# Conditioning tiles in buffers of their own, loaded two ahead and dealt out twice per block, in a two-layer encoder kernel; the first transfers in one queue; x times rstd formed once

## The chip, the core and the metric

The kernel runs on one core of a Trainium2 chip. The core has five engines with instruction streams of their own: TensorE (PE, matmul into the PSUM memory), VectorE (DVE), ScalarE (ACT), GpSimd (POOL) and SyncE (SP, which here only issues DMA transfers). Each works through its own list in order and waits for the others by semaphores. The metric is the time on the device of one execution, in microseconds (us). The kernel before took 959.88 us in the median of three runs (955.91 to 963.48).

## What is computed

A trunk of two layers over 256 tokens of width 1024. Each layer is half a gated feed-forward, a token mixer, and another half feed-forward; shift, scale and gate of each of the three norms come from one condition vector `c` by a matrix `mod_w` of 1024 x 9216 per layer:

```python
c_act = jax.nn.silu(c)
for i in range(DEPTH):                     # 2
    mod = (c_act @ mod_w[i] + mod_b[i])[:, None, :]
    sh0, sc0, g0, sh1, sc1, g1, sh2, sc2, g2 = jnp.split(mod, N_MOD, axis=-1)
    h = modulate(rms_norm(x, norm_g[i, 0]), sh0, sc0)      # h * (1 + scale) + shift
    x = x + 0.5 * g0 * swiglu(h, ffn_w_gu[i, 0], ffn_w_down[i, 0])
    h = modulate(rms_norm(x, norm_g[i, 1]), sh1, sc1)
    ...                                    # layer 0: pooling mixer, layer 1: differential attention
    x = x + g1 * y
    h = modulate(rms_norm(x, norm_g[i, 2]), sh2, sc2)
    x = x + 0.5 * g2 * swiglu(h, ffn_w_gu[i, 1], ffn_w_down[i, 1])
return rms_norm(x, final_g)
```

`swiglu` multiplies by a 1024 x 5632 matrix, takes `silu(g) * u`, and multiplies by a 2816 x 1024 matrix. All is float32.

## The kernel before

The activations stay on the chip, transposed: `xT` holds x as eight row blocks of 128 channels by 256 tokens. All weights are streamed once, in 312 units of 128 x 1024 (48 of them 128 x 768) in the order of use. A float32 product is made of three fast ones: each unit is split by ACT into a rounded part `hi` (L285) and by DVE into the remainder `lo` (L286), as are the activations (`hh`, `hl`, or `ah`, `al`), and `prod3` (L305 to L307) adds hi x hi, hi x lo and lo x hi in PSUM.

**The order of the work.** `split_unit` issues the load of a unit on SP's queue into the pool `rawp` (six raw buffers) and splits it; `unit` keeps five units ahead of the one in use, and there are seven buffers each for `hi` and `lo`. The instructions are placed on each engine by a scheduler at build time that goes by priority and by when it reckons inputs to be ready; on the chip each engine then follows that order.

**The conditioning.** The product of `c` with `mod_w` is done by DVE, in 144 tiles of 128 rows (`gemv_tile`, L243): a tile is loaded into a raw buffer of the same pool `rawp` (L247), and one instruction multiplies it with `cact` (silu of c in every partition) and sums each row into a column of `mod` (L248), followed by a short read-out of the sum. `mod_done` adds the bias and forms what the norm or the residual needs: `A` (scale with the norm's gain), `sh`, or the gate `G`. Eight tiles make one part of 1024 columns, 18 parts in all. Parts (0, 0) and (0, 1), shift and scale of the first norm, are made in the opening stage, row block by row block. The others are dealt out by `Background`: `tick` is called once per block of the up projection (11 blocks of 256 columns of gate and of up) and once per unit of the down projection, and does as many tiles as are then due.

**The stages.** The opening stage (L781 to L812) forms the first norm and, for each row block k, a tile of scale, a tile of shift, the normalised block, and the products with two units of 128 x 768 for the first three up blocks (`early`). Then come: feed-forward (0, 0) with its remaining eight up blocks and its down projection, the pooling mixer, feed-forwards (0, 1) and (1, 0), attention, feed-forward (1, 1). A down projection runs in four quarters of 256 output columns, six units each; after a quarter, `residual` (L372, then L314 and L315 for the scaled and split x of the next norm) and `squares` (L382, L383) add to x and to the sum of squares `acc`. At the start of a feed-forward or of attention `rstd_rows` sums `acc` over partitions on PE (L353). The first up blocks there do not wait for the norm: they multiply by x times gain, `xh` and `xl` (L408 to L410), and the factor `rstd` comes afterwards.

In this text the boundary after a down projection is where PE goes over to those products; the first of the two that the trace singles out lies between feed-forwards (0, 1) and (1, 0), the second between (1, 0) and attention.

Of the kernel before, what the change touches and what calls it, by code (L numbers as in the profile page):

```python
# [18 lines left out]
P = 128  # L19
# [11 lines left out]
RAW_BUFS = 6  # L31
SPLIT_BUFS = 7
LOOKAHEAD = 5
U_BUFS = 3
EARLY = 3

# [66 lines left out]

VECTORS = [("modb0", 72), ("ng0", 24), ("pscale", 8), ("modb1", 72), ("ng1", 24), ("fg", 8), ("subln", 1)]
# [32 lines left out]
def trunk(ctx: ExitStack, tc: tile.TileContext, x, c, mod_w, small, weights, diff_lambda, k_rope, out):  # L137
# [52 lines left out]
    for _ in range(10):  # L190
        PE.matmul(pt[:, :P], ones, ones, start=True, stop=True)
# [11 lines left out]


    cact = const([P, D], "cact")
# [9 lines left out]
    S.activation(cact, cact, AF.Silu)  # L215
# [5 lines left out]
    def mod_done(i, p, k0=0, k1=KD):  # L221

        n, ks = p // 3, slice(k0, k1)
        cs = slice(p * 8 + k0, p * 8 + k1)
# [6 lines left out]
        if key not in vecs:  # L231
            vecs[key] = const([P, KD], f"{key[0]}{i}{p}")
        v = vecs[key][:, ks]
        if p % 3 == 1:
            V.scalar_tensor_tensor(v, m, 1.0, vec[f"ng{i}"][:, n * 8 + k0:n * 8 + k1], ALU.add, ALU.mult)
        elif n != 1:
            V.tensor_scalar(v, m, 0.5, None, ALU.mult)
        elif i == 0:
            V.tensor_tensor(v, m, vec["pscale"][:, ks], ALU.mult)
        else:  # L240
            V.tensor_copy(v, m)

    def gemv_tile(i, p, k):  # L243

        raw = rawp.tile([P, D], F32, tag="raw", name=nm("raw"))
        r0 = (p * KD + k) * P
        nc.sync.dma_start(raw, mod_w[i, r0:r0 + P, :])  # L247
        V.scalar_tensor_tensor(raw, raw, 1.0, cact, ALU.mult, ALU.mult, accum_out=mod[i][:, p * KD + k:p * KD + k + 1])  # L248

    def gemv_steps(i, p):  # L250
        for k in range(KD):
            gemv_tile(i, p, k)
# [85 lines left out]
    def warm(f, after):  # L338

        S.activation(tiny(1, tag="warm", bufs=1), after, f, scale=0.0, bias=eps1)  # L340

# [48 lines left out]
    def normalise(js, rstd, a, b):  # L390

        with tc.high_priority(offset=100):
            for j in js:
                t = t1k()
                first = V.scalar_tensor_tensor(t, xT[:, j, :], a[:, j:j + 1], rstd, ALU.mult, ALU.mult)
                second = S.activation(hh[:, j, :], t, AF.Identity, bias=b[:, j:j + 1])
                V.scalar_tensor_tensor(hl[:, j, :], t, b[:, j:j + 1], hh[:, j, :].bitcast(F32), ALU.add, ALU.subtract)
        return first.ins, second.ins
# [56 lines left out]
    def ffn(i, s, ndef, nxt, parts_up, parts_down, early=()):  # L455
# [6 lines left out]
        back = Background(parts_up, KF // 2, ndef + len(early) // 2)  # L462
        for j in range(KF // 2):
            if (i, s, j) == (1, 0, 6):
                attention_consts()
            if j >= ndef:
# [37 lines left out]
            normalise(range(j * n, j * n + n), rstd, vecs["A", i, n3], b)  # L504
            back.tick()
# [274 lines left out]

    with tc.high_priority(offset=1000):  # L781
        pt = psmall()
        for half in range(2):
            sq = t1k(1024, "qk", 2)
            S.activation(sq, xT[:, 4 * half:4 * half + 4, :].rearrange(F), AF.Square)
            for k in range(4):
                PE.matmul(pt[:, :T], ones, sq[:, k * T:(k + 1) * T], start=(half + k == 0), stop=(half + k == 4))
        rstd = norm_of(pt, t1k(T, "pk", 1))
# [12 lines left out]
    on_v, on_s = scale_and_shift(0)  # L801
    for k in range(KD):
        with tc.issue_after(on_v), tc.issue_after(on_s):
            prefetch(2)
            if k < KD - 1:
                on_v, on_s = scale_and_shift(k + 1)
# [6 lines left out]
    ffn(0, 0, 0, ("A", 0, 1), [(0, 2), (0, 4), (0, 3), (0, 5)], [(0, 7), (0, 6)], early)  # L813
    pool_mixer(("A", 0, 2))
    ffn(0, 1, 2, ("A", 1, 0), [(0, 8), (1, 1)], [(1, 0), (1, 4)])
# [58 lines left out]
```

## Time and profile before

| what | value |
|---|---|
| median of three runs | 959.88 us (955.91 to 963.48) |
| the profiled execution | 959.34 us, of which 957.5 us are the span from first to last instruction |
| PE busy | 912.9 us, 95% of the span, 7504 matmuls |
| DVE busy | 743.9 us, 78% |
| ACT busy | 492.2 us, 51% |
| mean granted clock of PE | 0.982 |
| read from memory, mean rate | 234.86 MB, 249 GB/s with the writes |

Busy shares are means over stages with different limits; PE's matmuls are pipelined, so that a busy PE shows only that it always had one in flight. The granted clock is given as a share of 2.4 GHz; its two levels here are 1.00 and 0.50 (1.2 GHz). In rows of waits, the part before the arrow waited for the part behind it. In rows in order of time, the bracket gives the idle time ahead of the instruction and what ended it.

### The profile page before, as it was taken

The numbers are of one execution on the slowest core, as the hardware profiler recorded it, in microseconds if no ns is written. First come the engines' busy times: TensorE is split into PE (matmuls) and PEld (weight loads), VectorE is DVE, ScalarE is ACT, GpSimd is POOL, SyncE is SP. The second block draws the span as 40 slices with busy tenths as digits, with TensorE's granted clock in tenths as the row PEclk, the third lists the DMA queues.
The fourth block names the chain that finished last, engine by engine and source line by source line (L and its number), as shares of the span: only waits on it lengthen the run. The fifth ranks groups of instructions, "written<-read, shape, count | busy, mean of one in ns | idle before, by whom it ended". The sixth has DMA issues, their size and how long they took to land.

```text
span 957.5 us, 18703 instructions
## 1 busy us (share of the span) xinstructions
PE 912.9 (95%) x7504; PEld 898.8 (94%) x7504; DVE 743.9 (78%) x1238; ACT 492.2 (51%) x745; POOL 0.7 (0%) x6
## 2 busy tenths in 40 slices
PE   5999999998999999997999999969999999999997
PEld 4889999998999999997999999859999999999996
DVE  4899988898998666787997767688988897665551
ACT  3364444546745444355654434347777674444541
POOL 0000000000000000000000000000000000000000
PEclk7999999999999999998999999979999999999999
DMA  6989998997569878887698887894543448776621
GB/s 253 322 315 359 363 333 308 362 328 261 176 234 365 261 240 266 276 300 237 215 339 300 291 280 249 272 310 147 161 142 121 154 155 286 240 228 199 182 78 45
DMA packets 68583, 238.18 MB, mean 249 GB/s; under 512 B 7952, under 2 KB 9232, under 8 KB 68368
## 3 DMA queue, kind: packets, MB, share of 16 engines
q1 hardware_dynamic: 68208, 235.41, 72.1%
q8 instruction: 59, 0.97, 0.4%
q10 hardware_dynamic: 288, 1.57, 0.4%
q14 instruction: 28, 0.23, 0.1%
HBM read 234.86 MB, written 1.05 MB: 246 GB/s over the span
## 4 chain that ended last, share of the span: by engine, by line
PE 72%; DMA 12%; DVE 10%; issue 5%; ACT 1%; DVEq 0%; ACTq 0%
PE mm L305 17%; PE mm L307 17%; PE mm L306 16%; DMA raw<-in_mod_w_dram 10%; DVE lo L286 4%; PE hd L305 3%; PE hd L307 3%; PE hd L306 3%; PE mm L409 2%; PE mm L410 2%; PE mm L408 2%; DVE raw L248 2%; PE hd L618 1%; DMA raw<-in_weights_dram 1%; DMA xT<-in_x_dram 1%
## 5 line engine op out<-in xcount | busy, mean ns | idle before, releaser
L285 ACT ACTIVATE hi<-raw 128x1024 fp32r<-128x1024 f32 (+1 forms) x312 | 315.7, 1024 | 265.2 <-PE mm L306 108.3
L286 DVE TENSOR_TENSOR lo<-raw,hi 128x1024 fp32r<-128x1024 f32 (+1 forms) x312 | 362.9, 1180 | 69.6 <-ACT hi L285 66.9
L305 PE MATMUL mm<-hh,hi 128*128 128x256 f32 x992 | 277.8, 281 | 0.0
L306 PE MATMUL mm<-hl,hi 128*128 128x256 f32 x992 | 277.6, 281 | 0.0
L307 PE MATMUL mm<-hh,lo 128*128 128x256 f32 x992 | 275.8, 281 | 0.0
L248 DVE SCALAR_TENSOR_TENSOR raw<-raw,cact 128x1024 f32<-128x1024 f32 x144 | 174.3, 1222 | 79.8 <-DMA raw<-in_mod_w_dram 79.5
L307 PE MATMUL mm<-ahl,lo 128*128 128x256 f32 x768 | 216.1, 281 | 5.1 <-DVE lo L286 5.1
L305 PE MATMUL mm<-ahl,hi 128*128 128x256 f32 x768 | 215.6, 281 | 0.0
L306 PE MATMUL mm<-ahl,hi 128*128 128x256 f32 x768 | 215.3, 280 | 0.0
L305 PEld LDWEIGHTS mm<-hh,hi 128*128 128x128 f32 x992 | 186.7, 188 | 0.8
L306 PEld LDWEIGHTS mm<-hl,hi 128*128 128x128 f32 x992 | 186.9, 189 | 0.0
L307 PEld LDWEIGHTS mm<-hh,lo 128*128 128x128 f32 x992 | 185.9, 189 | 0.3
L307 PEld LDWEIGHTS mm<-ahl,lo 128*128 128x128 f32 x768 | 144.6, 188 | 6.6 <-DVE lo L286 6.5
L305 PEld LDWEIGHTS mm<-ahl,hi 128*128 128x128 f32 x768 | 144.6, 188 | 0.3 <-DVE xT L372 0.2
L306 PEld LDWEIGHTS mm<-ahl,hi 128*128 128x128 f32 x768 | 144.7, 188 | 0.0
L305 PE MATMUL hd<-hh,hi 128*128 128x256 f32 x288 | 81.5, 283 | 4.5 <-ACT hi L285 4.3
L307 PE MATMUL hd<-hh,lo 128*128 128x256 f32 x288 | 82.1, 285 | 3.5 <-DVE lo L286 3.2
L306 PE MATMUL hd<-hl,hi 128*128 128x256 f32 x288 | 81.1, 282 | 0.0
L410 PE MATMUL mm<-xh,lo 128*128 128x258 f32 x208 | 60.2, 291 | 1.9 <-DVE lo L286 1.9
L409 PE MATMUL mm<-xl,hi 128*128 128x256 f32 x208 | 61.4, 296 | 0.2 <-DVE xl L315 0.2
L408 PE MATMUL mm<-xh,hi 128*128 128x258 f32 x208 | 59.9, 291 | 0.1
L305 PEld LDWEIGHTS hd<-hh,hi 128*128 128x128 f32 x288 | 54.5, 189 | 5.7 <-ACT hi L285 5.7
(190 smaller groups left out, 1022.2 us busy)
## 6 DMA issues: line engine op xcount, KB each, us to landing
raw<-in_weights_dram SPq DMA_DIRECT2D x264, 512.0 KB, 4.8
raw<-in_mod_w_dram SPq DMA_DIRECT2D x144, 512.0 KB, 5.4
raw<-in_weights_dram SPq DMA_DIRECT2D x48, 384.0 KB, 4.6
xT<-in_x_dram ACTq DMA_DIRECT2D x1, 1024.0 KB, 8.3
out_dram<-u SPq DMA_DIRECT2D x4, 256.0 KB, 2.4
cact<-in_c_dram ACTq DMA_DIRECT2D x1, 512.0 KB, 4.7
pk<-qk SPq DMA_DIRECT2D x16, 32.0 KB, 2.8
qk<-pk SPq DMA_DIRECT2D x16, 32.0 KB, 1.8
```

Of the source, the lines that this page charges most:

```text
L248: V.scalar_tensor_tensor(raw, raw, 1.0, cact, ALU.mult, ALU.mult, accum_out=mod[i][:, p * KD + k:p * KD + k + 1])
L285: S.activation(hi[:, :w], raw[:, :w], AF.Copy)
L286: V.tensor_tensor(lo[:, :w], raw[:, :w], hi[:, :w].bitcast(F32), ALU.subtract)
L305: PE.matmul(o, lh, rh, start=start, stop=False, **kw)
L306: PE.matmul(o, lh, rl, start=False, stop=False, **kw)
L307: PE.matmul(o, ll, rh, start=False, stop=stop, **kw)
L408: PE.matmul(o[:, :T + 2], hi[:, kk, cs], xh[:, k, :], start=(k == 0), stop=False)
L409: PE.matmul(o[:, :T], hi[:, kk, cs], xl[:, k, :], start=False, stop=False)
L410: PE.matmul(o[:, :T + 2], lo[:, kk, cs], xh[:, k, :], start=False, stop=(k == KD - 1))
L618: PE.matmul(sc[c2][:, q * T:(q + 1) * T], l[pr, 0, qs], r[pr, 1, :], start=(n == 0), stop=(n == 2))
```

## The change

- The loads of x (in two halves) and of `c` are issued on SP's queue ahead of all others; the small vectors go to ACT's queue instead. `warm` (an activation of one column, which makes the activation table load early) is called for Silu and for the reciprocal root in the opening.
- The matmuls on ones at the start are 12 instead of 10, and 12 more stand between the sum of squares and the first product.
- In the opening, x times rstd is formed once per block by DVE (`scaled_x`: one block, one, two, then four in one instruction); ACT forms the block's `A` and `sh` columns and twice the normalised block (`h` in full and `hh` rounded), and DVE subtracts. Before, DVE formed `A`, `sh` and `t`, ACT `hh`, and DVE the difference.
- Conditioning tiles have three buffers of their own (tag `cond`). `gemv_load` issues loads from one list of all tiles in the order of use, in the background up to two tiles beyond the one in use; in the opening a tile is loaded just when it is used.
- `Background` has 22 ticks per up projection instead of 11: one behind the gate product and one behind the up product of each block.
- The weights' pools shrink: five raw buffers instead of six, six `hi` and `lo` buffers instead of seven, four units ahead instead of five.

```diff
-RAW_BUFS = 6
-SPLIT_BUFS = 7
-LOOKAHEAD = 5
+RAW_BUFS = 5
+SPLIT_BUFS = 6
+LOOKAHEAD = 4
+COND_BUFS = 3
+WARM = 12
...
     cact = const([P, D], "cact")
-    nc.scalar.dma_start(cact, c.broadcast_to([P, D]))
-    nc.scalar.dma_start(xT, x)
+    for half in range(2):
+        hs = slice(half * KD // 2, (half + 1) * KD // 2)
+        nc.sync.dma_start(xT[:, hs, :], x[:, hs, :])
+    nc.sync.dma_start(cact, c.broadcast_to([P, D]))
...
-    nc.sync.dma_start(vecT, small)
+    nc.scalar.dma_start(vecT, small)
...
+    tiles = iter([(0, p, k) for k in range(KD) for p in (1, 0)] + [(*part, k) for part in PARTS for k in range(KD)])
+    loaded = []
+
+    def gemv_load(n):
+        while len(loaded) < n:
+            nxt = next(tiles, None)
+            if nxt is None:
+                return
+            i, p, k = nxt
+            raw = rawp.tile([P, D], F32, tag="cond", name=nm("cond"), bufs=COND_BUFS)
+            r0 = (p * KD + k) * P
+            nc.sync.dma_start(raw, mod_w[i, r0:r0 + P, :])
+            loaded.append((nxt, raw))
+
+    def gemv_tile(i, p, k, out, ahead_=COND_BUFS):
 
-        raw = rawp.tile([P, D], F32, tag="raw", name=nm("raw"))
-        r0 = (p * KD + k) * P
-        nc.sync.dma_start(raw, mod_w[i, r0:r0 + P, :])
-        V.scalar_tensor_tensor(raw, raw, 1.0, cact, ALU.mult, ALU.mult, accum_out=mod[i][:, p * KD + k:p * KD + k + 1])
+        gemv_load(ahead_)
+        which, raw = loaded.pop(0)
+        assert which == (i, p, k)
+        return V.scalar_tensor_tensor(raw, raw, 1.0, cact, ALU.mult, ALU.mult, accum_out=out)
...
-        back = Background(parts_up, KF // 2, ndef + len(early) // 2)
+        back = Background(parts_up, KF, 2 * ndef + len(early))
...
                     mm_rows(pg, hh, hl)
+                back.tick()
                 S.activation(w[:, :512], pg, AF.Silu)
...
     def scale_and_shift(k):
+        ks = slice(k, k + 1)
         for p in (1, 0):
-            gemv_tile(0, p, k)
-            mod_done(0, p, k, k + 1)
-        return normalise([k], rstd, vecs["A", 0, 0], mod[0][:, 0:8])
+            last = gemv_tile(0, p, k, d[:, p, ks], 1)
+        S.activation(a0[:, ks], d[:, 1, ks], AF.Identity, scale=ng[:, ks], bias=b1[:, ks])
+        S.activation(sh0[:, ks], d[:, 0, ks], AF.Identity, bias=vec["modb0"][:, ks])
+        xk = xr[k // 4][:, k % 4 * T:(k % 4 + 1) * T]
+        h = t1k()
+        with tc.high_priority(offset=100):
+            S.activation(h, xk, AF.Identity, scale=a0[:, ks], bias=sh0[:, ks])
+            second = S.activation(hh[:, k, :], xk, AF.Identity, scale=a0[:, ks], bias=sh0[:, ks])
+            third = V.tensor_tensor(hl[:, k, :], h, hh[:, k, :].bitcast(F32), ALU.subtract)
+        return last.ins, second.ins, third.ins
```

**SP's queue at the start of the program.** Before, it opens with the small vectors and two conditioning tiles (`raw` from `in_mod_w`), then two weight units; x and c are issued by ACT at that time:

```order
L210 DMA vecT<-in_small_dram 128x209
L247 DMA raw_139<-in_mod_w_dram 128x1024
L247 DMA raw_145<-in_mod_w_dram 128x1024
L282 DMA raw_153<-in_weights_dram 128x768
L282 DMA raw_159<-in_weights_dram 128x768
L247 DMA raw_165<-in_mod_w_dram 128x1024
L247 DMA raw_170<-in_mod_w_dram 128x1024
```

In the changed kernel:

```order
L218 DMA xT<-in_x_dram 128x1024 x2
L219 DMA cact<-in_c_dram 128x1024
L268 DMA cond_166<-in_mod_w_dram 128x1024
L268 DMA cond_169<-in_mod_w_dram 128x1024
L310 DMA raw_178<-in_weights_dram 128x768
L310 DMA raw_184<-in_weights_dram 128x768
L268 DMA cond_191<-in_mod_w_dram 128x1024
L268 DMA cond_194<-in_mod_w_dram 128x1024
```

Three transfers have moved to the head of the queue, and one has left it.

**DVE ahead of the last residual of feed-forward (0, 1)**, the first of the two boundaries (`lo` are splits, `xT` is the residual of the last quarter, `raw` or `cond` with `mod` in the row is a conditioning product). Before:

```order
L248 SCALAR_TENSOR_TENSOR raw_5060,mod_106<-raw_5060,cact 128x1024
L248 SCALAR_TENSOR_TENSOR raw_5087,mod_106<-raw_5087,cact 128x1024
L286 TENSOR_TENSOR lo_5002<-raw_5000,hi_5001 128x1024
L226 TENSOR_TENSOR mod_106<-mod_106,vecT 128x8
L286 TENSOR_TENSOR lo_5032<-raw_5030,hi_5031 128x1024
L235 SCALAR_TENSOR_TENSOR A_5091<-mod_106,vecT 128x8
L286 TENSOR_TENSOR lo_5065<-raw_5063,hi_5064 128x1024
L286 TENSOR_TENSOR lo_5095<-raw_5093,hi_5094 128x1024
L286 TENSOR_TENSOR lo_5150<-raw_5148,hi_5149 128x1024
L372 SCALAR_TENSOR_TENSOR xT<-mm_4933,G_3689,xT 128x256 x2
```

In the changed kernel:

```order
L276 SCALAR_TENSOR_TENSOR cond_6115,mod_113<-cond_6115,cact 128x1024
L314 TENSOR_TENSOR lo_5021<-raw_5019,hi_5020 128x1024
L314 TENSOR_TENSOR lo_5051<-raw_5049,hi_5050 128x1024
L276 SCALAR_TENSOR_TENSOR cond_6183,mod_113<-cond_6183,cact 128x1024
L276 SCALAR_TENSOR_TENSOR cond_6186,mod_113<-cond_6186,cact 128x1024
L314 TENSOR_TENSOR lo_5084<-raw_5082,hi_5083 128x1024
L241 TENSOR_TENSOR mod_113<-mod_113,vecT 128x8
L314 TENSOR_TENSOR lo_5114<-raw_5112,hi_5113 128x1024
L276 SCALAR_TENSOR_TENSOR cond_6251,mod_113<-cond_6251,cact 128x1024
L314 TENSOR_TENSOR lo_5169<-raw_5167,hi_5168 128x1024
L396 SCALAR_TENSOR_TENSOR xT<-mm_4952,G_3708,xT 128x256 x2
```

Four products stand in this quarter instead of two, spread among the five splits instead of ahead of them; they belong to feed-forward (1, 0).

**DVE ahead of the last residual of feed-forward (1, 0)**, the second boundary. Before:

```order
L248 SCALAR_TENSOR_TENSOR raw_7421,mod_106<-raw_7421,cact 128x1024
L248 SCALAR_TENSOR_TENSOR raw_7448,mod_106<-raw_7448,cact 128x1024
L286 TENSOR_TENSOR lo_7363<-raw_7361,hi_7362 128x1024
L226 TENSOR_TENSOR mod_106<-mod_106,vecT 128x8
L286 TENSOR_TENSOR lo_7393<-raw_7391,hi_7392 128x1024
L286 TENSOR_TENSOR lo_7426<-raw_7424,hi_7425 128x1024
L286 TENSOR_TENSOR lo_7454<-raw_7452,hi_7453 128x1024
L286 TENSOR_TENSOR lo_7506<-raw_7504,hi_7505 128x1024
L372 SCALAR_TENSOR_TENSOR xT<-mm_7294,G_5884,xT 128x256 x2
```

In the changed kernel:

```order
L314 TENSOR_TENSOR lo_7382<-raw_7380,hi_7381 128x1024
L314 TENSOR_TENSOR lo_7412<-raw_7410,hi_7411 128x1024
L314 TENSOR_TENSOR lo_7445<-raw_7443,hi_7444 128x1024
L314 TENSOR_TENSOR lo_7473<-raw_7471,hi_7472 128x1024
L314 TENSOR_TENSOR lo_7525<-raw_7523,hi_7524 128x1024
L396 SCALAR_TENSOR_TENSOR xT<-mm_7313,G_5903,xT 128x256 x2
```

The two products in front are gone; the five splits and the residual remain in their order.

## Rows read from the trace of the kernel before

**Rows 1.** The span, from the head of the page.

```profile
span 957.5 us, 18703 instructions
```

**Rows 2.** Stretches, PE alone, then all: busy (instructions), PEclk, DMA share, GB/s.

```profile
10.00:16.00 6.00, 5.44 (x16) 0.65 1.03 406
16.00:20.00 4.00, 0.03 (x1) 1.00 0.04 15
...
20.00:62.00 42.00, 37.88 (x274) 34.66 (x275) 38.06 (x79) 16.75 (x25) 0.00 (x0) 0.96 0.90 313
62.00:151.00 89.00, 89.00 (x760) 89.00 (x760) 81.56 (x113) 44.53 (x54) 0.00 (x0) 1.00 0.95 347
```

**Rows 3.** The opening in order of time (start, length, instruction, idle before); x's landing.

```profile
10.56 5.47 PE L787 MATMUL st<-qk,ones 128*128 128x256 f32 x16 [5.67 <-ACT qk L785]
16.07 0.43 DVE L344 TENSOR_SCALAR t<-st 128x256 f32<-128x256 f32 x1 [4.00 <-PE st L787]
20.18 0.39 PE L305 MATMUL hd<-hh,hi 128*128 128x256 f32 x1 [4.14 <-ACT hi L285]
59.31 2.96 DVE L286 TENSOR_TENSOR lo<-raw,hi 128x768 fp32r<-128x768 f32 x3 [0.25 <-ACT hi L285]
...
xT<-in_x_dram ACTq DMA_DIRECT2D x1, 1024.0 KB, 8.3
```

**Rows 4.** The first boundary in order of time, DVE and PE.

```profile
422.26 0.87 DVE L372 SCALAR_TENSOR_TENSOR xT<-mm,G,xT 128x256 f32<-128x256 f32 x2
431.63 3.49 DVE L286 TENSOR_TENSOR lo<-raw,hi 128x1024 fp32r<-128x1024 f32 x3
435.03 0.87 DVE L372 SCALAR_TENSOR_TENSOR xT<-mm,G,xT 128x256 f32<-128x256 f32 x2
...
431.92 0.28 PE L408 MATMUL mm<-xh,hi 128*128 128x258 f32 x1
438.16 1.22 PE L353 MATMUL st<-acc,ones 128*128 128x256 f32 x2 [5.95 <-DVE acc L383]
```

**Rows 5.** DVE's waits for tiles, 376 to 438 us, then whole; a tile's median landing.

```profile
DVE raw L248 <- DMA raw<-in_mod_w_dram: 13.2, 9, 2.8
...
DVE raw L248 <- DMA raw<-in_mod_w_dram: 79.5, 50, 4.2
...
raw<-in_mod_w_dram SPq DMA_DIRECT2D x144, 512.0 KB, 5.4
```

**Rows 6.** PE's waits, 262 to 660, then 62 to 220: total, times, longest.

```profile
PE st L353 <- DVE acc L383: 13.0, 2, 7.1
PE mm L307 <- DVE lo L286: 3.3, 3, 1.3
PE mm L410 <- DVE lo L286: 1.9, 1, 1.9
...
PE mm L307 <- DVE lo L286: 1.8, 3, 1.0
```

**Rows 7.** Stretches behind the boundaries, columns as in the second of rows 2.

```profile
438.20:444.20 6.00, 6.00 (x26) 5.82 (x27) 3.14 (x8) 1.08 (x2) 0.00 (x0) 0.50 0.81 305
446.20:452.20 6.00, 6.00 (x53) 6.00 (x52) 4.01 (x9) 2.99 (x5) 0.00 (x0) 1.00 0.58 178
641.70:645.40 3.70, 3.70 (x15) 3.52 (x16) 2.74 (x7) 0.42 (x1) 0.00 (x0) 0.50 0.87 355
```

**Rows 8.** DVE's groups by shape: busy, mean ns of one; its busy time 445 to 570.

```profile
L286 DVE TENSOR_TENSOR lo<-raw,hi 128x1024 fp32r<-128x1024 f32 x264 | 318.2, 1221 | 58.6 <-ACT hi L285 55.9 <-DMA pk<-qk 1.7
L248 DVE SCALAR_TENSOR_TENSOR raw<-raw,cact 128x1024 f32<-128x1024 f32 x144 | 174.3, 1222 | 79.8 <-DMA raw<-in_mod_w_dram 79.5
L286 DVE TENSOR_TENSOR lo<-raw,hi 128x768 fp32r<-128x768 f32 x48 | 45.1, 954 | 11.1 <-ACT hi L285 11.0
L372 DVE SCALAR_TENSOR_TENSOR xT<-mm,G,xT 128x256 f32<-128x256 f32 x44 | 19.4, 478 | 17.0 <-PE mm L307 17.0
...
445.00:570.00 125.00, 102.13 (x157) 1.00 0.81 274
```

More of the change, by code (lines that the diff above doesn't have):

```diff
@@ L101, in unit_shape @@
     return (ix[-2].stop - ix[-2].start) // P, ix[-1].stop - ix[-1].start
+UP = [[(0, 2), (0, 4), (0, 3), (0, 5)], [(0, 8), (1, 1)], [(1, 2), (1, 3), (1, 5)], [(1, 8)]]
+DOWN = [[(0, 7), (0, 6)], [(1, 0), (1, 4)], [(1, 7), (1, 6)], []]
+PARTS = [part for up, down in zip(UP, DOWN) for part in up + down]
 VECTORS = [("modb0", 72), ("ng0", 24), ("pscale", 8), ("modb1", 72), ("ng1", 24), ("fg", 8), ("subln", 1)]
@@ L189, in trunk @@
     pt = psum()
-    for _ in range(10):
+    for _ in range(WARM):
         PE.matmul(pt[:, :P], ones, ones, start=True, stop=True)
@@ L394, in normalise @@
                 t = t1k()
[L395 to L396 removed]
+                V.scalar_tensor_tensor(t, xT[:, j, :], a[:, j:j + 1], rstd, ALU.mult, ALU.mult)
+                S.activation(hh[:, j, :], t, AF.Identity, bias=b[:, j:j + 1])
                 V.scalar_tensor_tensor(hl[:, j, :], t, b[:, j:j + 1], hh[:, j, :].bitcast(F32), ALU.add, ALU.subtract)
[L398 removed]
     def mm_deferred(os_):
@@ L504, in ffn @@
             normalise(range(j * n, j * n + n), rstd, vecs["A", i, n3], b)
+            back.tick()
             back.tick()
@@ L777, in attention @@
                     normalise((j, j + 1), rstd, vecs["A", 1, 1], b)
+    xr = [t1k(1024, "qk", 2) for _ in range(2)]
     with tc.high_priority(offset=1000):
@@ L787, in trunk, with scaled_x @@
                 PE.matmul(pt[:, :T], ones, sq[:, k * T:(k + 1) * T], start=(half + k == 0), stop=(half + k == 4))
+        idle = psmall()
+        for _ in range(WARM):
+            PE.matmul(idle[:, :P], ones, ones, start=True, stop=True)
         rstd = norm_of(pt, t1k(T, "pk", 1))
-    early = [psum2(), psum2()] + [psum() for _ in range(2 * EARLY - 2)]
+    def scaled_x(k0, k1):
+        n, o = k1 - k0, k0 % 4 * T
+        V.tensor_tensor(xr[k0 // 4][:, o:o + n * T].rearrange("p (k t) -> p k t", k=n), xT[:, k0:k1, :],
+                        rstd.rearrange("p (o t) -> p o t", o=1).broadcast_to([P, n, T]), ALU.mult)
+    with tc.high_priority(offset=1000):
+        scaled_x(0, 1)
+    early = [psum2(), psum2()] + [psum() for _ in range(2 * EARLY - 2)]
+    b1, d = const([P, KD], "b1"), const([P, 2, KD], "d")
+    a0 = vecs["A", 0, 0] = const([P, KD], "A00")
+    sh0 = vecs["sh", 0, 0] = mod[0][:, 0:KD]
+    ng = vec["ng0"][:, 0:KD]
+    V.scalar_tensor_tensor(b1, vec["modb0"][:, KD:2 * KD], 1.0, ng, ALU.add, ALU.mult)
     def scale_and_shift(k):
+        ks = slice(k, k + 1)
         for p in (1, 0):
-            gemv_tile(0, p, k)
-            mod_done(0, p, k, k + 1)
-        return normalise([k], rstd, vecs["A", 0, 0], mod[0][:, 0:8])
-    on_v, on_s = scale_and_shift(0)
+            last = gemv_tile(0, p, k, d[:, p, ks], 1)
[8 more added lines that the diff above has]
+        return last.ins, second.ins, third.ins
+    on_v, on_s, after = scale_and_shift(0)
     for k in range(KD):
```

41 lines of the change are left out of this document (22 added, 19 removed).

## The prediction

> **What bounds the kernel now.** I read the span first [rows 1], then TensorE's (PE's) waits, because everything in the program ends up feeding it. PE is the bound almost everywhere: from 62 to 151 us it is busy in all of the 89 us and issues 760 matmuls, one per 0.117 us, at full clock [rows 2]. What can be won lies where PE stands still or runs at its lower clock level, and that is in few places.
>
> The first is the start. PE does its first useful product at 20.18 us, and the last weights of the opening stage are split only at about 61 us (the stretch at 59.31 us holds three splits of 0.96 us, of which two belong to that stage) [rows 3]. DMA, the loads of that stage, runs at 406 GB/s from 10 to 16 us, then almost stops (15 GB/s) until 20 us, and afterwards moves 313 GB/s [rows 2]: the six raw buffers are full and nothing frees them until the norm is there. The norm is late because x is: its transfer takes 8.3 us to land, and VectorE (DVE) then waits 4.00 us for PE's sum of squares until 16.07 us [rows 3].
>
> The others are the two boundaries at which a down projection ends, and the down projections before them. At the first, PE stops at 432.2 and waits 5.95 us for the sum of squares; the chain of DVE shows why: the residual of the previous quarter ran at 422.26 us, then came two conditioning products (which wait for their DMA), and five splits, so that the last residual began at 435.03 us, although PE had its input ready before 432 us [rows 4]. The time DVE lost there is the waiting for conditioning tiles: 13.2 us in 9 waits from 376 to 438 us [rows 5]. A tile of `mod_w` takes a raw buffer of the weights' pool and is used by DVE right behind its load in program order, so DVE stands for most of the 5.4 us of its landing [rows 5]. At the second boundary PE waits 1.9 and 7.1 us, and three times before it, 3.3 us together [rows 6]. After each boundary PE's granted clock is 0.50, its level of 1.2 GHz: 26 matmuls in 6.0 us instead of 53 is a loss of 6.0 x 27/53 = 3.0 us; at the second, 15 in 3.7 us instead of 33, 2.0 us [rows 7]. So 5.95 + 3.0 = 9.0 us hang on the first boundary, 1.9 + 7.1 + 2.0 = 11.0 us on the second, 3.3 us on the waits between, and 1.8 us on three short waits in the first down projection [rows 6].
>
> **The start, part by part.** Moving x and c ahead of all else in SP's queue puts 1.57 MB first; the small vectors move to ScalarE's (ACT's) queue, where their only early reader (one 128x8 operation of DVE) stands ahead of a product that cannot begin before about 8 us anyway. A 512 KB tile takes 5.4 us to land [rows 5], so I put the second half of x at 6 us instead of 9.4. ACT squares, PE adds (5.5 us, at the half clock [rows 2, 3]) and the ACT table of the reciprocal root is now loaded before it is asked for. The norm chain and the first product come 3.5 to 5 us earlier. Then DVE's work per row block shrinks: `t` (0.48 us, like the other 256-wide products) and three tiny operations go eight times; four multiplies of x by rstd come, 0.48 us for a 256-wide one, at most 1.22 us for the widest, 2.6 us in all [rows 8]. Counting starts and not ends, since neighbours overlap by some 0.07 us, that is 8 x 0.6 - 2.6 = 2.2 us less. ACT gets three small operations per block, but is busy in 16.75 of 42 us there [rows 2]. Together 5.7 to 7.2 us. The loads allow it: 16.4 MB are needed by the end of the stage, which at 347 GB/s [rows 2] takes 47 us, ending near 50 and not 58. I take **-6.5**, between -2 (if the loads go on at the rate of now and only the standstill shrinks) and -10 (the whole standstill and all of DVE's saving).
>
> The twelve extra matmuls on ones between the squares and the first product, and the two of the start-up, stand where PE is idle now (16 to 20 us, 0.03 us busy [rows 2]): nothing.
>
> A rule of the Trainium skill speaks against the queue part: the page "DMA: Bandwidth & Descriptors", section "Issuing engines are not separate DMA queues", says that transfers of all issuing engines run on the same 16 DMA engines and interleave, so the choice of queue only moves issue time. By that alone x would land where it does now, the start would give some 3 us, and the whole would come to 937 us. No run here shows it; I hold to the order of issue, because x now shares those engines with six loads that SP issues beside it.
>
> **The conditioning tiles.** They get three buffers of their own and are loaded up to two ahead, dealt out per half block. The number of products stays 144 and the bytes stay. The order shows that they run ahead: behind the opening's 16, the numbers that DVE does with the weights of up and down of the four feed-forwards were 24, 20 | 15, 15 | 24, 16 | 8, 0 and become 28, 19 | 24, 19 | 30, 5 | 0, 0 (the rest in the mixers). The last quarter of the third down projection has none any more, so the second boundary and the three waits before it lose their cause: **-10** of 11.0 (bounds -5, if five splits in front of the residual are late for other reasons, and -11) and **-3** of 3.3 (bounds 0 and -3.3).
>
> The first boundary is less sure, as four products now stand in its last quarter instead of two. A quarter of DVE's work: four 1024-wide splits, two 768-wide, and six 256-wide operations, 4 x 1.22 + 2 x 0.95 + 6 x 0.48 = 9.7 us, and 1.3 us per product with its read-out (1.22 and a little) [rows 8]: 14.9 us with four, 16.2 with five, less 1.2 us of overlap. PE needs 132 x 0.117 = 15.4 us. So DVE fits, with 0.4 to 1.7 us to spare, if its waits of 13.2 us in four quarters [rows 5] go; loaded two ahead, a tile has two products' distance (some 6.5 us) against 5.4 us of landing. I take **-7.5** of 9.0 (bounds 0 and -9.0). The short waits of the first down projection: **-1** (0 to -1.8).
>
> **What is given back.** One raw and one split buffer less means weights only four units ahead instead of five, some 11 us of PE work, still twice the landing. In the first up projection the loads are near their limit: eight half-megabyte loads (4.2 MB) in a block of 96 x 0.117 = 11.2 us are 374 GB/s, against 347 GB/s measured there at a DMA share of 0.95 and 406 GB/s at the best [rows 2]. Starting it earlier leaves less in hand. I allow **+2** (0 to 8).
>
> Sum: -6.5 - 1 - 7.5 - 3 - 10 + 2 = -26 on the span of 957.5 us: 931.5, and 1.84 us lie outside the span in that run (959.34, by 0.5 us below the median 959.88): 933.3, given as **933.5 us**.
>
> **Rivals.** *x lands no earlier.* If transfers issued later overtake the two halves of x as those beside it do now, the norm stays at 18 us and the start gives DVE's 2.2 us and some 0.8 from the extra buffers: 937. For it: 8.3 us for 1 MB now; against it: the later ones are now issued behind it. *The loads set the opening.* If 347 GB/s is what DMA gives, the 28 products and 32 units of the first up projection, 60 x 0.524 = 31.5 MB, take 90.7 us where 56 took 84.6, and 6 of the 6.5 us go back: 939. For it: share 0.95; against it: 406 GB/s before. *The first boundary stays.* Nineteen products in that down projection instead of 15 keep DVE late: 933.5 + 7.5 = 941; with waits of 2 us a quarter it would come so. *The waits move along.* The change doesn't do what it says: SP issues in order, a load of weights that waits for one of five raw buffers holds the tile's load behind it, and DVE waits as now, only elsewhere; with the start alone, 953. Against it: the tiles no longer need a raw buffer. *Slower*: the products drawn ahead into the second feed-forward (24 + 19 where 30 were) wait there for DMA by 1.5 us each. At the mean wait of now, 13.2/9 = 1.5 us [rows 5], a quarter of its down projection costs DVE 13.6 + 4.75 x 1.5 = 20.7 against PE's 15.4 us; four quarters lose 21 us where 9.0 were lost, and the third up projection with 30 products another 30 x 1.5 less its slack of 23 us (DVE is busy in 102 of 125 us there [rows 8]), 22 us more: 959 less the 21 of the other terms, plus 12 and 22, is 972. It turns slower at about 1.25 us a product (16 - 9 + 14.5 = 21.5); it needs loads two ahead to gain nothing, which the 5.4 us of landing speak against.
>
> **Chances.** The forecast 0.56 (its own range 922 to 941), x no earlier 0.06, the loads 0.12, the boundary 0.13, moved along 0.07, slower 0.06. Low end: every term at its far bound without the give-back is -10 - 1.8 - 9 - 3.3 - 11 = -35, 924, and 922 with a margin for the pool mixer; high end 948, the two middle rivals together. A change of 1% is about what a measurement of this kernel can tell: faster 0.85, same 0.09, slower 0.06.
>
> **What would show it.** First useful product near 15 to 16 us and no standstill of DMA at 16 to 20; block 3 starting some 6 us sooner; DVE's waits for `mod_w` well under half of 79.5 us [rows 5]; no wait of PE at the second boundary, at most 2 us at the first; clock 1.00 behind both. I am wrong if the waits of PE on splits appear in the second or third feed-forward, if DVE's waits for tiles stay, or if the opening ends where it did.

## The result, and the profile after

The changed kernel takes 951.06 us in the median of 20 runs (947.03 to 958.03), the kernel before 959.77 (952.87 to 963.48); the ratio is 0.992, with a 95% interval of 0.990 to 0.994. The change gains 8.7 us, where 26 were forecast, and lies above the forecast range. The profiled execution took 958.03 us, the longest of them; a second profile of the same kernel (e11, below) took 950.73 us and shows the same waits, so both are used.

The stretches of [rows 2], in the changed kernel (PE, PEld, DVE, ACT, POOL busy with their instructions, PEclk, DMA share, GB/s):

```profile
10.00:16.00 6.00, 2.72 (x25) 2.52 (x23) 4.33 (x9) 3.53 (x8) 0.00 (x0) 0.90 0.98 353
16.00:20.00 4.00, 2.93 (x12) 2.64 (x12) 3.90 (x8) 2.70 (x6) 0.00 (x0) 0.50 0.86 280
20.00:62.00 42.00, 37.62 (x289) 36.77 (x290) 35.08 (x53) 26.73 (x47) 0.00 (x0) 0.94 0.90 311
62.00:151.00 89.00, 86.82 (x725) 85.40 (x724) 79.28 (x111) 40.74 (x48) 0.00 (x0) 1.00 0.93 341
```

The standstill of DMA from 16 to 20 us is gone (280 GB/s instead of 15). But in the first up projection, where PE had been busy without a break, it now does 725 matmuls instead of 760. The opening in order of time, then x's landing among the DMA issues (KB each, median us), answer to [rows 3]:

```profile
6.32 3.72 PE L813 MATMUL st<-u,ones 128*128 128x256 f32 x16 [0.65 <-ACT u L811]
16.86 0.58 PE L333 MATMUL hd<-hh,hi 128*128 128x256 f32 x1 [4.14 <-ACT hi L313]
54.75 0.58 ACT L846 ACTIVATE hh<-qk,mod,A 128x256 fp32r<-128x256 f32 x1
...
10.46 1.23 DVE L276 SCALAR_TENSOR_TENSOR cond<-cond,cact 128x1024 f32<-128x1024 f32 x1 [4.84 <-DMA cond<-in_mod_w_dram]
11.61 0.42 DVE L368 TENSOR_SCALAR t<-st 128x256 f32<-128x256 f32 x1
```

```profile
xT<-in_x_dram SPq DMA_DIRECT2D x2, 512.0 KB, 5.0
```

The sum of squares begins at 6.32 instead of 10.56 us and ends at 10.04 instead of 16.03; the first product comes at 16.86 instead of 20.18. The sum is 6.0 us earlier, the product only 3.3: DVE was in a conditioning product when the sum was ready and took it up at 11.61 us, and a second product (11.94 to 13.16 us) stands ahead of the rest of the norm. The first boundary, DVE and PE in order of time, then the stretch behind it, answer to [rows 4, 7]:

```profile
441.68 1.23 DVE L276 SCALAR_TENSOR_TENSOR cond<-cond,cact 128x1024 f32<-128x1024 f32 x1 [2.31 <-DMA cond<-in_mod_w_dram]
...
449.25 0.87 DVE L396 SCALAR_TENSOR_TENSOR xT<-mm,G,xT 128x256 f32<-128x256 f32 x2
...
452.37 1.22 PE L377 MATMUL st<-acc,ones 128*128 128x256 f32 x2 [10.02 <-DVE acc L407]
```

```profile
452.40:458.40 6.00, 6.00 (x26) 5.82 (x27) 3.91 (x10) 1.06 (x2) 0.00 (x0) 0.50 0.89 302
```

PE waits 10.02 us there, not 5.95 (7.87 in the second profile), again for DVE's last residual, and loses as much clock behind it. What DVE waits for, from 376 to 452 us and then whole, answers to [rows 5] (total, times, longest):

```profile
DVE cond L276 <- DMA cond<-in_mod_w_dram: 12.5, 11, 2.3
...
DVE cond L276 <- DMA cond<-in_mod_w_dram: 47.8, 41, 4.8
```

PE's waits from 440 to 700 us, to be set against [rows 6]:

```profile
PE st L377 <- DVE acc L407: 10.0, 1, 10.0
```

The whole run's waits for tiles fell from 79.5 to 47.8 us; behind about 600 us there are none, as the products have run out. At the first boundary they stayed: 12.5 us where 13.2 were. The second boundary is clean: the one row is all that PE waits from 440 to 700 us.

**Where the time went.** The sum over partitions (`st`) marks the end of a stage on PE. Its start in four profiled executions, in us, and the shift against before:

| start of the sum at | before | changed | changed again (e11) | e6 | forecast shift | shift in e11 |
|---|---|---|---|---|---|---|
| pooling mixer | 224.1 | 227.4 | 226.0 | 217.2 | -5.5 | +1.9 |
| feed-forward (0, 1) | 245.6 | 252.0 | 248.6 | 235.3 | -5.5 | +3.0 |
| first boundary | 438.2 | 452.4 | 445.4 | 421.0 | -13 | +7.2 |
| second boundary | 641.7 | 642.9 | 635.0 | 608.8 | -26 | -6.7 |
| end of the span | 957.5 | 956.2 | 948.9 | 923.1 | -26 | -8.6 |

The forecast shift adds the terms up to each place: -6.5, -1 and +2 by the mixer, -7.5 at the first boundary, -3 and -10 by the second (some 2.5 of the 7.5 and 2 of the 10 are lost clock, which lies behind the sum in its row). The two rows of e11 on which most hangs, PE in order of time:

```profile
226.01 0.50 PE L384 MATMUL st<-ones,acc 128*128 128x1 f32 x4
...
445.44 1.22 PE L377 MATMUL st<-acc,ones 128*128 128x256 f32 x2 [7.87 <-DVE acc L407]
```

Up to the first boundary the changed kernel loses 7 to 14 us instead of winning 13; from there to the second it wins 13 to 14 us, as forecast.

**What the trace says of the cause.** DMA issues on SP's queue from 402 to 408 us (start, length), then DVE's product that waits in between:

```profile
402.58 0.33 SPq L310 DMA_DIRECT2D raw<-in_weights_dram  x1
402.96 0.42 SPq L268 DMA_DIRECT2D cond<-in_mod_w_dram  x1
407.24 0.33 SPq L310 DMA_DIRECT2D raw<-in_weights_dram  x1
407.62 0.43 SPq L268 DMA_DIRECT2D cond<-in_mod_w_dram  x1
```

```profile
404.84 1.23 DVE L276 SCALAR_TENSOR_TENSOR cond<-cond,cact 128x1024 f32<-128x1024 f32 x1 [2.29 <-DMA cond<-in_mod_w_dram]
```

A tile's load (L268) goes out here 0.38 us behind a weight load (L310); the tile of the product at 404.84 us is one issued so at 397.87 us (below). What SP itself waited for from 376 to 452 us:

```profile
SPq L310 <- DVE lo L314: 45.0, 23, 4.8
SPq L310 <- DVE acc L407: 5.7, 4, 1.6
SPq L310 <- DVE mod L241: 5.0, 1, 5.0
```

All of it is at weight loads, which need a raw buffer that a split of DVE must free; SP never waits there for a tile's buffer. So a tile's buffer was free each time that SP came to its load, while SP waited for the weights in front. The chain of waits of this stretch goes round accordingly, split, weight load, tile load, split; pieces of two turns (start, length):

```profile
397.49 0.33 SPq L310
397.87 6.95 DMA cond<-in_mod_w_dram
...
407.24 0.33 SPq L310
407.62 6.90 DMA cond<-in_mod_w_dram
```

In the first feed-forward it is the other way round. SP's waits from 100 to 180 us:

```profile
SPq L268 <- DVE cond L276: 49.3, 15, 5.7
...
SPq L310 <- DVE lo L314: 3.9, 2, 2.0
```

There tiles are wanted faster, SP waits 49.3 us for a tile's buffer, and the loads of weights stand behind it; PE then waits 3.20 us at the change to the down projection (161.42 us). The theory from here on is called "in order": two streams of loads with buffers of their own in one queue hold each other up.

### The profile page after: what moved, and what is told of

Read it like the earlier page. It is cut to its first block, busy times and chain, and to the rows that moved or that the text cites. A ratio compares the mean times of both kernels' runs of the same rounds, so it can differ in the third digit from the quotient of the medians.

```text
span 956.2 us, 18740 instructions
## 1 busy us (share of the span) xinstructions
PE 913.8 (96%) x7532; PEld 900.8 (94%) x7532; DVE 742.8 (78%) x1211; ACT 502.4 (53%) x771; POOL 0.7 (0%) x6
## 4 chain that ended last, share of the span: by engine, by line
PE 66%; DMA 13%; DVE 11%; issue 4%; ACT 4%; SPq 1%; DVEq 0%; ACTq 0%
PE mm L335 16%; PE mm L333 16%; PE mm L334 16%; DMA cond<-in_mod_w_dram 12%; DVE lo L314 5%; DVE cond L276 3%; PE mm L431 2%; PE mm L433 2%; PE mm L432 2%; PE hd L333 2%; PE hd L335 2%; PE hd L334 2%; ACT hi L313 2%; DMA raw<-in_weights_dram 1%; PE hd L643 1%
## 5 line engine op out<-in xcount | busy, mean ns | idle before, releaser
L276 DVE SCALAR_TENSOR_TENSOR cond<-cond,cact 128x1024 f32<-128x1024 f32 x144 | 174.6, 1221 | 48.6 <-DMA cond<-in_mod_w_dram 47.8
```

The source lines that it names most:

```text
L276: return V.scalar_tensor_tensor(raw, raw, 1.0, cact, ALU.mult, ALU.mult, accum_out=out)
```

## The experiments

**e1: the tiles' loads in a queue of their own**, with the products held at their places in DVE's order (`PIN` is the number of splits that stand ahead of each in the changed kernel).

```diff
-            nc.sync.dma_start(raw, mod_w[i, r0:r0 + P, :])
+            (nc.gpsimd if n > 1 else nc.sync).dma_start(raw, mod_w[i, r0:r0 + P, :])
...
+        behind = PIN.pop(0)
+        with tc.issue_after(lows[min(behind, len(lows)) - 1]):
+            V.scalar_tensor_tensor(raw, raw, 1.0, cact, ALU.mult, ALU.mult, accum_out=out)
```

> The changed kernel, with one thing different: the background loads of conditioning tiles are issued on GpSimd's queue, which carries no other work, instead of SP's. The conditioning products are held at the places in VectorE's order that they have in the changed kernel (by number of splits ahead of them). Theory 'in order': in SP's queue a tile's load stands behind a weight load that waits for a raw buffer, so it is issued late although its own buffer is free; then the waits of the products for their tiles from 376 to 452 us fall from 12.5 us to under 4, over the whole run from 47.8 to under 20 us, PE's wait at the first boundary falls from 10.0 us to under 3, and the time is 938 to 944. Rival 'too much in one place': VectorE and DMA simply have too many products in the second feed-forward; then the waits and the boundary stay as they are, and the time is 948 to 954. Rival 'one buffer less': the weights, four ahead instead of five, are what is late; then the waits for tiles fall, but waits of PE on splits stay, and the time is 947 to 953.

Measured: 942.06 us (931.62 to 943.75; before 960.6), ratio 0.978 (0.972 to 0.985). DVE's waits for background tiles over the whole run, a new wait of PE, and the landing of a tile:

```profile
DVE cond L281 <- DMA cond<-in_mod_w_dram: 10.3, 14, 1.7
```

```profile
264.75 0.58 PE L341 MATMUL mm<-hh,lo 128*128 128x256 f32 x1 [7.00 <-DVE lo L320]
```

```profile
cond<-in_mod_w_dram POOLq DMA_DIRECT2D x128, 512.0 KB, 6.1
```

From 376 us to the first boundary no product waits for its tile, and PE does not wait at the boundary. A tile lands no faster (6.1 us, against 6.2 in the changed kernel): it is issued earlier. The same 19 products stand in this down projection, so it was not their number that held PE up in the changed kernel. "In order" holds. Nine us came back (the profile is of the fastest of the four runs, 931.62 us; the others took 940.87 to 943.75), and a wait of 7.00 us at the start of the second feed-forward came to light.

**e2: the new opening alone; e3: the tiles' part alone.** In e2 `RAW_BUFS`, `SPLIT_BUFS`, `LOOKAHEAD` are 6, 7, 5, tiles use tag `raw` and are loaded at use, one tick per block; e3 is the changed kernel with the opening, the first transfers and `normalise` of before.

> The new opening alone: transfers in one queue, x times rstd once, the warm activations and matmuls. Conditioning tiles take raw buffers of the weights' pool at their use, one tick per block, six raw and seven split buffers, all as in the kernel before. The prediction put this part at -6.5 us: 953. If what the opening gains is given back in the first up projection, because the loads are the limit there: 957 to 960. If the opening is nearly all of what the change gained: 950 to 952, and then the tiles alone bring nothing.

> The tiles' part alone: own buffers, loads up to two ahead, ticks twice per block, five raw and six split buffers, with the opening of the kernel before. The prediction put this part at -19.5 us: 940. Theory 'in order': the second boundary and the waits before it go (about -14), the first boundary grows by some 4 us and a few waits appear in the second feed-forward, so 953 to 957. Rival 'one buffer less' with the loads at their limit: the first up projection loses as well, 956 to 962.

Measured: e2 953.91 us (950.62 to 957.17), ratio 0.992 (0.990 to 0.995); e3 960.35 us (956.20 to 964.52), ratio 1.000 (0.997 to 1.004), both beside 960.6 of before. The opening gave what was forecast for it; the tiles gave nothing at all, a little worse than "in order" had it. PE's waits in e3 from 235 to 300 us and from 448 to 700:

```profile
PE mm L331 <- DVE lo L310: 7.0, 1, 7.0
...
PE st L373 <- DVE acc L403: 10.0, 1, 10.0
```

The second boundary is clean here too, but the 7.0 us of e1 at the start of the second feed-forward and the 10.0 us at the first boundary take it back.

**e4: one tick per block.**

```diff
-        back = Background(parts_up, KF, 2 * ndef + len(early))
+        back = Background(parts_up, KF // 2, ndef + len(early) // 2)
...
-                back.tick()
```

> The changed kernel with one tick per block of the up projection instead of two, all else kept. The products then stand in groups of two to four, at nearly the same places on the whole. Theory 'in order': what decides is the queue, so the time stays within 3 us of the changed kernel: 948 to 954. Rival 'dealing decides': products standing in groups again wait for their loads one after the other, VectorE's waits for tiles rise from 48 towards 80 us, and the time goes to 956 to 960.

Measured: 956.30 us (947.59 to 961.26), ratio 0.995 (0.992 to 0.998), which overlaps with the changed kernel's. Waits for tiles are 49.6 us, where the rival wanted towards 80. The time fell between the two expectations: whether dealing twice brings a few us is open; it is not where the gain went.

**e5 and e6: products held at their ticks**, with the loads on SP's queue (e5) and on GpSimd's (e6).

```diff
+        with tc.issue_after(lows[-1]):
+            V.scalar_tensor_tensor(raw, raw, 1.0, cact, ALU.mult, ALU.mult, accum_out=out)
```

> The changed kernel with its loads in SP's queue, and each conditioning product held behind the split last issued at its tick, so that products are no longer drawn ahead of the block at which they are due (20 to 24 of them stand in each feed-forward's later part again, and 8 in the last). Theory 'in order' (e1): the queue decides; the products still wait for tiles whose loads stand behind weight loads, 45 to 80 us in all, and with 16 products in the third down projection again the second boundary's wait of PE comes back, 2 to 7 us; time 949 to 957. Rival 'drawn ahead': what cost the changed kernel its gain are the products that stand too early in the second feed-forward; then the first boundary's wait falls from 10.0 to under 6 us and the time is 940 to 946 without another queue.

> As e5, with the background tiles' loads on GpSimd's queue as in e1. Together with the changed kernel, e1 and e5 this makes all four pairs of queue and places. 'In order': waits for tiles under 20 us, no wait of PE over 2 us at either boundary. In e1 PE waited 7.0 us for a split at 264.75 us, at the start of the second feed-forward, where VectorE was full with products drawn ahead; with the products held that wait should go, which is 7 us and 1 to 2 us of clock: 933 to 939 against 942 of e1. If that wait had another cause it stays, and the time is 940 to 944; if 16 products in the third down projection make VectorE late at the second boundary even with their tiles there, 942 to 948.

Measured: e5 950.94 us (947.75 to 954.19), ratio 0.992 (0.989 to 0.995); e6 925.14 us (924.03 to 925.85), ratio 0.965 (0.962 to 0.968), before 958.73. The four pairs:

| | loads on SP's queue | in a queue of their own |
|---|---|---|
| products where the scheduler drew them | 951.1 | 942.1 |
| products held at their ticks | 950.9 | 925.1 |

The kernel before, measured beside them, took 959.77 us (changed), 960.6 (e1) and 958.73 (e5, e6); against it the four gain 8.7, 18.5, 7.8 and 33.6 us, which is the same picture. Both parts are needed: the queue alone brings 9 us, the places alone nothing, both 26. PE's waits in e6 over the whole run:

```profile
PE hd L337 <- ACT hi L317: 5.6, 3, 3.6
PE hd L339 <- DVE lo L318: 2.8, 5, 1.1
PE mm L197 <- DVE eps L200: 1.1, 1, 1.1
PE st L388 <- DVE acc L411: 1.0, 1, 1.0
```

Nothing is left at the boundaries, nor of the 7.00 us: that wait was DVE's own work, products that stood too early. The gain is larger than the 933 to 939 us expected, and e6 beats both kernels, the one before by 3.5%. In e5 the expectation from "in order" failed in its details: all of DVE's waits for tiles in the whole run are one in the opening (L278), where 45 to 80 us were expected in the background, and PE waits at neither boundary, where 2 to 7 us were expected at the second. The sign of the rival "drawn ahead" came (the first boundary's wait under 6 us), its time of 940 to 946 us did not:

```profile
DVE cond L278 <- DMA cond<-in_mod_w_dram: 4.3, 1, 4.3
```

So holding the products alone already ends the waits for tiles in the background. That e5 gains nothing all the same shows the coupling's other side. The stretch from 100 to 180 us in the changed kernel, in e5 and in e6, then SP's waits there in e5:

```profile
100.00:180.00 80.00, 74.05 (x604) 72.23 (x603) 67.10 (x97) 37.28 (x44) 0.00 (x0) 0.98 0.94 345
```

```profile
100.00:180.00 80.00, 69.91 (x563) 66.90 (x561) 63.96 (x92) 31.63 (x39) 0.00 (x0) 1.00 0.88 309
```

```profile
100.00:180.00 80.00, 80.00 (x682) 80.00 (x681) 72.55 (x105) 36.89 (x46) 14.26 (x27) 1.00 0.96 355
```

```profile
SPq L269 <- DVE cond L280: 50.9, 21, 4.7
```

A held product frees its tile's buffer later; with one queue, the weights behind that load are later too, and PE does 563 matmuls instead of 682. The sum ahead of the mixer in e5 begins at 239.6 us, 13.6 later than in e11; from the next sum to the end it then takes 684.9 us (264.0 to 948.9) where e11 takes 700.3 (248.6 to 948.9), so the gain of the places is there and was paid for in advance.

**e7: two parts dealt out elsewhere.** `UP[1]` is `[(0, 8), (1, 1), (1, 0)]`, `DOWN[1]` `[(1, 2)]`, `UP[2]` `[(1, 4), (1, 3), (1, 5)]`.

> As e6, with two parts dealt out elsewhere: part (1, 0) in the up projection of the second feed-forward and (1, 2) in its down projection instead of (1, 0) and (1, 4) there, (1, 4) in the next up projection, so that the down projection before the first boundary has 8 products instead of 16. VectorE then has about 5 us less to do per two quarters there. If VectorE's load at the first boundary still matters in e6, this is 2 to 6 us faster than e6: 931 to 936. If the queue was all, the same as e6 within 2 us.

Measured: 926.12 us (918.75 to 928.25), ratio 0.965 (0.960 to 0.970), the same as e6: once tiles are there in time and the products are held, DVE's load at the first boundary no longer matters.

**e8: no loads of tiles in the background.**

```diff
-        return V.scalar_tensor_tensor(raw, raw, 1.0, cact, ALU.mult, ALU.mult, accum_out=out)
+        V.scalar_tensor_tensor(kept[-2], kept[-1], 1.0, cact, ALU.mult, ALU.mult, accum_out=out)
```

> The changed kernel without the background loads of conditioning tiles: from the first feed-forward on, all 128 products read one tile that is already there and write to another; the shift, scale and gate vectors are therefore not those of the reference. Products stand at their places in the changed kernel; VectorE's and PE's work is the same, 67 MB less are loaded. It bounds what any earlier arrival of tiles can bring. 'In order': about what e1 gives, 938 to 944, since in e1 nearly all tiles came in time. If the traffic of the tiles also costs (weights landing later, DMA's share 0.9 in the first up projection), 928 to 937. If tiles were not the cause, 948 or more.

Measured: 928.53 us (925.85 to 932.76), ratio 0.969 (0.965 to 0.973). So in the changed kernel the tiles' loads cost about 22 us in all. The time lies in the range put down for a cost of their traffic, not in that of "in order" alone. What is left of PE's waits beyond the opening:

```profile
259.69 0.58 PE L342 MATMUL mm<-hh,lo 128*128 128x256 f32 x1 [6.39 <-DVE lo L321]
```

With no tile to wait for, the wait at the start of the second feed-forward stands: it comes from where the products are, not from loads. e1, with these places and all loads in their own queue, is 13.5 us slower in the median, though its profiled execution (span 929.8 us) is not: what its other executions lose, and whether the traffic is the cause, no profile shows. e6, with all loads, is 3.4 us faster than e8, but its products are held, and no run has held products without loads. From 100 us on PE waits in e6 for 1.5 us in all, so with the products held the traffic leaves little to see.

**e9: e6 with the opening of before; e10: e6 with x and c on ScalarE's queue** and the small vectors on SP's, as before (x whole). In both, the opening's conditioning products are held at given places too. The edit of e10:

```diff
-        nc.sync.dma_start(xT[:, hs, :], x[:, hs, :])
-    nc.sync.dma_start(cact, c.broadcast_to([P, D]))
+    nc.scalar.dma_start(cact, c.broadcast_to([P, D]))
+    nc.scalar.dma_start(xT, x)
```

> As e6 (925.1 us), with the opening of the kernel before: x and c on ScalarE's queue, no warm activations or extra matmuls, x times gain times rstd formed per row block by VectorE. It weighs the opening in a kernel in which little else waits. The prediction's term of 6.5 us would make it 931 to 932. In the trace of the changed kernel the first product comes 3.3 us earlier and the last row block of the opening also 3.3 us earlier, none of which is added by VectorE's smaller share per block: by that, 928 to 929. If the loads are the limit behind the opening and take the gain back: 925 to 926.

> As e6, with the first transfers alone as before: x whole and c on ScalarE's queue, the small vectors on SP's; the rest of the new opening stays. If the order in one queue is what brings x earlier, the first product moves back by 2 to 3.3 us and the time is 927 to 929. If transfers of both queues share the same engines and the choice of queue changes nothing, x lands as in e6 and the time is 925 to 926.

Measured beside 925.14 us of e6: e9 933.12 us (932.78 to 933.60), e10 929.11 us (927.70 to 931.81). The first product in e6, then in e10, and x's landing in e10:

```profile
16.52 0.39 PE L337 MATMUL hd<-hh,hi 128*128 128x256 f32 x1 [3.56 <-ACT hi L317]
```

```profile
22.53 0.39 PE L337 MATMUL hd<-hh,hi 128*128 128x256 f32 x1 [2.79 <-ACT hi L317]
```

```profile
xT<-in_x_dram ACTq DMA_DIRECT2D x1, 1024.0 KB, 8.4
```

By the times the opening is worth 8.0 us and the order of the first transfers 4.0. (The kernel before took 960.0 us beside these two and 958.73 beside e6; set against that they are 6.7 and 2.7.) The sum ahead of the mixer, in e6, e9 and e10, then PE's pace behind it in e6 and in e9:

```profile
217.23 0.61 PE L388 MATMUL st<-ones,acc 128*128 128x1 f32 x4 [0.99 <-DVE acc L411]
221.14 0.61 PE L386 MATMUL st<-ones,acc 128*128 128x1 f32 x4 [1.67 <-DVE acc L409]
221.52 0.60 PE L388 MATMUL st<-ones,acc 128*128 128x1 f32 x4 [1.25 <-DVE acc L411]
```

```profile
300.00:400.00 100.00, 100.00 (x852) 100.00 (x851) 77.41 (x103) 47.17 (x59) 10.56 (x20) 1.00 0.85 281
300.00:400.00 100.00, 100.00 (x845) 100.00 (x844) 76.58 (x104) 47.54 (x59) 10.03 (x19) 1.00 0.84 282
```

e10 is 4.3 us behind e6 at the mixer and 4.1 at the end of the span (927.2 and 923.1 us): its loss is all in the opening. e9 is 3.9 us behind at the mixer and 8.5 at the end (931.6): half of its loss comes later, with hardly a wait of PE, which does fewer matmuls there in the same time; what sets that no run shows. So by the mixer the whole new opening brings no more than its first transfers alone. On the other queue x lands later: ACT squares its halves from 5.38 and 6.69 us in e6, both from 9.55 us in e10. The rule that I had weighed (the Trainium skill, "DMA: Bandwidth & Descriptors", section "Issuing engines are not separate DMA queues": the transfers of all engines share the same 16 DMA engines and interleave) fits this: x on a queue beside SP's interleaved with SP's loads, and came later for it. What it makes of the choice of queue, only a small saving of issue time, does not hold here: 4.0 us for x, and 9 to 26 us for the tiles.

**e11 and e12: second profiles** of the changed kernel and of e2.

> The changed kernel unchanged, for a second profile: the one shown is 958.0 us, near the slow end of its runs, whose median is 951.1. If the new waits (about 10 us at the first boundary, 3 us at the change from up to down projection in the first feed-forward, 2 us at the start of the second) belong to the kernel, they stand here too; if they belong to that one run, they are shorter by 5 us or more in sum.

> The kernel of e2 unchanged, for a second profile. In the profile of e2, the matmuls from 280 to 420 us followed one another every 0.112 us (179 in 20 us) where all other stretches of all kernels have 0.116 (172 in 20 us), at the same granted clock, which makes some 6 us of its gain over the kernel before. If that pace belongs to the kernel, it stands here at the same place; if it falls by chance, it stands elsewhere or nowhere, and the gain of the opening read at the end of the first feed-forward (1.5 us) is nearer to what the opening does.

Measured: e11 950.73 us, with 7.87 us at the first boundary, 3.08 at the change to the first down projection and 2.28 at the start of the second feed-forward: they belong to the kernel. e12 954.92 us. The stretch from 300 to 320 us in e2 and in e12:

```profile
300.00:320.00 20.00, 20.00 (x179) 20.00 (x178) 14.99 (x21) 9.35 (x11) 0.00 (x0) 1.00 0.95 344
```

```profile
300.00:320.00 20.00, 20.00 (x172) 20.00 (x171) 15.25 (x23) 9.77 (x12) 0.00 (x0) 1.00 0.85 281
```

The faster pace of e2 isn't the kernel's, and the time without it is nearly the same (954.9). The sum ahead of the mixer begins at 222.6 us in e2 and at 220.7 in e12, 1.5 and 3.4 us earlier than before.

## Why the prediction was wrong, point by point

**The start (-6.5): right in its size, only in part for its reason.** Alone it gives 6.7 us (e2), in e6's surroundings 6.7 to 8.0 (e9). But by the sum ahead of the mixer the profiles show 1.5 us (e2), 3.4 (e12) and 3.9 (e9 against e6); the rest comes in later stages, which this term does not speak of, and that it makes up the 6.5 is luck. What there is comes from the first transfers (4.3 us in e10). The 2.2 us of DVE's smaller share per block did not show: the last row block of the opening is normalised at 54.75 us instead of 58.03, the same 3.3 us earlier as the first product. That was 3.3 where 3.5 to 5 were expected, as two conditioning products stand in DVE's part of the norm. Nor was there a table load to save: before, ACT loaded it at 11.47 us and used it at 16.53.

**The first boundary (-7.5): wrong, and the step that failed** is "loaded two ahead, a tile has two products' distance (some 6.5 us) against 5.4 us of landing". Buffers for two tiles ahead are not loads two ahead. A load's lead begins when SP comes to it, and SP comes to it only when the weight load in front has its raw buffer, that is after a split on DVE, the same engine that then waits for the tile: from 376 to 452 us SP spent 55.7 of 76 us waiting in front of weight loads, and DVE 12.5 us waiting for tiles; with the tiles' loads in their own queue (e1) DVE's waits there went to nothing and PE's with them. I had read the places on DVE from the order of instructions, but not SP's, although the prediction itself says that each queue is in order: the rival "the waits move along", with this mechanism and 953 us, got a chance of 0.07, against it stood "the tiles no longer need a raw buffer". That is true and beside the point. PE's wait grew from 5.95 to 10.02 (7.87) us: DVE lost nearly as much as before (12.5 us where 13.2 were) and had 19 products to do instead of 15, some 5 us more. Of the four in the last quarter three waited, 0.20, 2.31 and 0.45 us. One row was misread as well: DVE did not stand for "most of the 5.4 us" of a landing, but for 1.5 us in the mean and 2.8 at most in that stretch [rows 5].

**The first feed-forward (-1 and, of the +2, most): wrong for the same cause.** In e11 the sum ahead of the mixer comes 1.9 us later than before, where 5.5 us earlier was forecast. It is not DMA's rate, as the give-back and the rival "the loads set the opening" had it: e6 reads 355 GB/s there with the same buffers, and PE does not wait. So one raw and one split buffer less cost nothing that shows there either.

**The second boundary and the three waits before it (-10 and -3): right.** From the first boundary's sum to the second's the changed kernel takes 190.5 us instead of 203.5, in e11 189.6, which is 13 to 14 us less.

**The rival "slower"** named the products drawn ahead into the second feed-forward. That mechanism is there (7.00 us in e1, 6.39 in e8 without any load), but as work of DVE at the start of the stage rather than a wait of 1.5 us per product. Its sum is off too: a quarter with 4.75 products is 9.7 + 4.75 x 1.3 - 1.2 = 14.7 us, where 13.6 stands, so that it should have come out some 4 us slower still.

The misses of the forecast, from the table: 7.4 us by the mixer, 1.1 in it, 11.7 from there to the first boundary, and 2.8 better behind it; together the 17.4 us between 931.5 and e11's span of 948.9.

What stays open: why the first boundary's wait differs by 2 us from run to run, what e1 loses in the executions that were not profiled, where the part of the start's gain comes from that no profile shows by the mixer, and whether e4's ticks cost anything.

## What to carry to other kernels

Here two streams of loads with buffers of their own stayed coupled by the one queue that issued them in order: each load went out only after the waits in front of it. Before crediting a prefetch with its buffers' depth, look in the trace at what the issuing engine waits for ahead of that load; if it is the other stream's buffer, give the stream a queue of an engine that does nothing else, and hold its consumers where they are due, since the scheduler here drew them forward into a stage that had no room (7.00 us in e1).

## What the runs showed that I had not expected

PE has more than one pace at the same granted clock of 1.00: 172 or 179 matmuls in 20 us, one per 0.116 or 0.112 us. The faster one held through whole stretches of single executions (from about 272 to 400 us in e2's profile, from about 776 us to near the end in e1's) and was not there in the second profile of e2's kernel (e12). What it is worth depends on who else is waited for: in e1 the last part, from the sum at 742.5 us to the end, takes 187.3 us where e6 takes 193.0, but in e2 the stage up to the first boundary takes 191.5 us where e12 takes 193.2, as PE then waits longer (9.5 us against 7.2). A smaller difference, 845 or 852 matmuls in 100 us, stands between e9 and e6. So PE's pace may account for part of the spread between runs of one kernel; what sets it no run here shows.
